# A 2x2 average pool: SP's load queue gets the first turn, and the last tile comes in two parts instead of three

## The chip, the cores and the metric

The kernel runs on one core of a Trainium2 chip. The metric is the device time of one execution in microseconds (us), lower is better. A kernel is executed several times. One of the executions is profiled, and its time is among those listed; the kernel before was profiled in an execution of its own (3104.99 us), which is in no list. The chips of the measurements differ and are told apart below as chips A to D (and the first measurement, whose chip is not named). The clock of the matrix engine, which is unused here, was granted at 1.0.

The engines are named as in the profile: DVE (VectorE) adds, ACT (ScalarE) scales and issues loads, POOL (GpSimd) issues stores, SP (SyncE) issues loads. Transfers run on 16 DMA engines, whoever issues them. A transfer waits in the queue of the engine that issued it; a *turn* is the time in which one DMA engine moves one piece (one packet) of one queue; and a transfer *lands* on a DMA engine when that engine reports its share as done.

## The reference, cut to what matters

```python
x: [32, 128, 256, 256] float32, kernel_size 2, stride 2
output[:, :, i, j] = mean over the 2x2 window of x          # [32, 128, 128, 128]
```

1073.7 MB are read and 268.4 MB written. There are three additions and one scaling per output.

## The kernel before

The input is 128 tiles of 32 "units" (a unit is two input rows per partition). A tile is loaded in two halves: SP loads its even partitions, ACT its odd ones, each 4 MB, one run of 65,536 bytes per partition. There are two tile buffers. DVE adds twice, ACT scales, and POOL stores two finished tiles at a time. Cuts are marked.

```python
    parts, a = [], 0
    while a < rest:                                  # rest is 32: the last tile
        b = rest if rest - a <= 8 else a + (rest - a) // 2
        parts.append((a, b, sem(f"part{len(parts)}")))   # 16, 8 and 8 units
        a = b

    def load(odd, k, b):
        (act if odd else sp).dma_start(out=ins[b][odd::2], in_=xp[b, odd][k]).then_inc(loaded[b], 16)
    ...
        for b in range(2):                           # SP
            load(0, 0, b)
        with sp.Fori(1, pairs) as k:
            for b in range(2):
                take(sp, free[b])
                load(0, k, b)
    ...
        for a, b, part in parts:                     # DVE, the last tile
            take(dve, part, 32)
            sums(it[:, a:b], dst[:, a:b])
    ...
        for b in range(2):                           # ACT
            load(1, 0, b)
        with act.Fori(0, (pairs - 1) // 2) as i:
            for c in range(2):
                for b in range(2):
                    next_load(b, load, 2 * i + (c + 1), b)
                    scale(both[c][:, b], scaled)
    ...
        for a, b, _ in parts:                        # ACT, the last tile
            take(act, summed)
            scale(dst[:, a:b], done)
            take(act, done)
            act.dma_start(out=block(...)[1], in_=dst[:, a:b]).then_inc(tail, 16)
```

Of the kernel before, what the change touches and what calls it, by code (L numbers as in the profile page):

```python
# [9 lines left out]
@with_exitstack  # L10
def kernel(
    ctx: ExitStack,
    tc: tile.TileContext,
    x: bass.AP,
    kernel_size: bass.AP,
    stride: bass.AP,
    out: bass.AP,
):
    nc = tc.nc
    P = nc.NUM_PARTITIONS  # L20

    n, c, h, w = x.shape
    k = int(kernel_size)
    s = int(stride)
    h_out = (h - k) // s + 1
    w_out = (w - k) // s + 1
    R = n * c * h_out
    units = R // P if R % P == 0 else 0


    if k == 2 and s == 2 and h % 2 == 0 and w == 256 and units >= 1024 and (units - 1) // 64 % 2 and (units - 1) // 32 % 2:
        _pool_2x2(ctx, tc, x, out, units)
    else:
        _generic_pool(ctx, tc, x, out, k, s, n, c, h, w, h_out, w_out)
# [5 lines left out]
def _pool_2x2(ctx, tc, x, out, units):  # L40
    nc = tc.nc
    P = nc.NUM_PARTITIONS
    f32 = mybir.dt.float32
    w = x.shape[3]
    w_out = w // 2
    sp, act, dve, pool = nc.sync, nc.scalar, nc.vector, nc.gpsimd

    xv = x.rearrange("n c (ho a) w -> (n c ho) (a w)", a=2)
    ov = out.rearrange("n c ho wo -> (n c ho) wo")









    in_pool = ctx.enter_context(tc.tile_pool(name="inp", bufs=2))
    out_pool = ctx.enter_context(tc.tile_pool(name="outp", bufs=2))  # L60
    ins = [in_pool.tile([P, TILE, 2 * w], f32, name="in_tile") for _ in range(2)]
    both = [out_pool.tile([P, 2, TILE, w_out], f32, name="res") for _ in range(2)]
    res = [both[t // 2][:, t % 2] for t in range(4)]

    def sem(name):
        return ctx.enter_context(nc.semaphore(name))

    loaded, free, stored, emptied = [
        [sem(f"{n}{b}") for b in range(2)] for n in ("loaded", "free", "stored", "emptied")
    ]  # L70
    halfway, summed, scaled, held, done, tail = [
        sem(n) for n in ("halfway", "summed", "scaled", "held", "done", "tail")
    ]



    def take(engine, sem, n=1):
        engine.wait_ge(sem, n)
        engine.sem_inc(sem, -n)  # L79

    def block(r0, g):
        rows = slice(r0, r0 + g * P)
        return xv[rows].rearrange("(p g) f -> p g f", p=P), ov[rows].rearrange("(p g) f -> p g f", p=P)

    pairs, rest = divmod(units - TILE - 1, 2 * TILE)
    whole, rest = 2 * pairs + 1, rest + 1
    assert pairs % 2 and pairs >= 5 and rest <= TILE
    last = 2 * pairs * TILE * P
    xp = xv[0:last].rearrange("(k o p t g) f -> t o k p g f", o=2, t=2, p=P // 2, g=TILE)
    op = ov[0:last].rearrange("(k o p g) f -> o k p (g f)", o=2, p=P // 2, g=2 * TILE)  # L90
    parts, a = [], 0
    while a < rest:
        b = rest if rest - a <= 8 else a + (rest - a) // 2
        parts.append((a, b, sem(f"part{len(parts)}")))
        a = b

    def load(odd, k, b):
        (act if odd else sp).dma_start(out=ins[b][odd::2], in_=xp[b, odd][k]).then_inc(loaded[b], 16)

    def load_block(odd, dst, r0, g, landed):  # L100
        (act if odd else sp).dma_start(out=dst[odd::2], in_=block(r0, g)[0][odd::2]).then_inc(landed, 16)

    def load_last(odd):
        for a, b, part in parts:
            load_block(odd, ins[whole % 2][:, a:b], (whole * TILE + a) * P, b - a, part)

    def sums(it, dst):
        dve.tensor_add(out=it[:, :, 0:w], in0=it[:, :, 0:w], in1=it[:, :, w:]).then_inc(halfway)  # L108
        take(dve, halfway)
        dve.tensor_add(out=dst, in0=it[:, :, 0:w:2], in1=it[:, :, 1:w:2]).then_inc(summed)  # L110

    def tile_sums(t):
        if t % 2 == 0:
            take(dve, emptied[t // 2 % 2])
        take(dve, loaded[t % 2], 32)
        sums(ins[t % 2], res[t % 4])

    def scale(dst, sem):
        act.mul(out=dst, in_=dst, mul=0.25).then_inc(sem)  # L119

    def next_load(b, *what):

        take(act, summed)
        act.sem_inc(free[b])
        what[0](1, *what[1:])



    def store_from(engine, k, c, landed):
        for o in range(2):  # L130
            src = both[c][o::2].rearrange("p t g f -> p (t g f)")
            engine.dma_start(out=op[o][k], in_=src).then_inc(landed, 16)  # L132

    def store(k, c):
        take(pool, scaled, 2)
        store_from(pool, k, c, stored[c])

    def emptied_by(c, landed):
        pool.wait_ge(stored[c], landed)
        pool.sem_inc(emptied[c])  # L140

    with tc.tile_critical():

        for b in range(2):
            load(0, 0, b)
        with sp.Fori(1, pairs) as k:
            for b in range(2):
                take(sp, free[b])
                load(0, k, b)
        take(sp, free[0])  # L150
        load_block(0, ins[0], last, TILE, loaded[0])
        take(sp, free[1])
        load_last(0)
        take(sp, held, 2)
        c = (pairs - 1) % 2
        store_from(sp, pairs - 1, c, tail)


        for b in range(2):
            dve.sem_inc(emptied[b])  # L160
        with dve.Fori(0, whole // 4):
            for t in range(4):
                tile_sums(t)
        for t in range(whole - whole % 4, whole):
            tile_sums(t)
        it = ins[whole % 2]
        dst = ins[(whole + 1) % 2].rearrange("p g (s f) -> p (g s) f", s=4)[:, 0:TILE]
        for a, b, part in parts:
            take(dve, part, 32)
            sums(it[:, a:b], dst[:, a:b])  # L170


        for b in range(2):
            load(1, 0, b)
        with act.Fori(0, (pairs - 1) // 2) as i:
# [4 lines that stand above are left out]
        c = (pairs - 1) % 2  # L180
        next_load(0, load_block, ins[0], last, TILE, loaded[0])
        scale(both[c][:, 0], held)
        next_load(1, load_last)
        scale(both[c][:, 1], held)
        take(act, summed)
        scale(res[(whole - 1) % 4], done)
        take(act, done)
        act.dma_start(out=block(last, TILE)[1], in_=res[(whole - 1) % 4]).then_inc(tail, 16)
        for a, b, _ in parts:
# [3 lines that stand above are left out]
            act.dma_start(out=block((whole * TILE + a) * P, b - a)[1], in_=dst[:, a:b]).then_inc(tail, 16)  # L193


        store(0, 0)
        with pool.Fori(0, (pairs - 3) // 2) as i:
            for c in (1, 0):
                store(2 * i + (2 - c), c)
                emptied_by(1 - c, 32 * i + 32)  # L200
        store(pairs - 2, 1)
        for c in range(2):
            emptied_by(c, 16 * (pairs - 1))
        pool.drain()


        take(sp, tail, 16 * (len(parts) + 3))
# [95 lines left out]
```

## Time and profile before

| | before |
|---|---|
| time, median of the first 3 executions | 3107.12 us (3106.73 to 3108.3) |
| profiled execution, its span | 3104.99 us, 3103.3 us |
| DVE, ACT, POOL busy | 54%, 16%, 2% |
| DMA | 90% or more in each of 40 slices, mean 433 GB/s |

The prediction below shows the lines for this, those of the timeline with start, duration, engine, line, operation, operands, idle time before it. The page's list of DMA queues names the queue, its packets, its megabytes, and its share of the 16 engines' time; q1 is SP's queue, q10 ACT's, and q0 the software queue of POOL:

```profile
q10 hardware_dynamic: 10976, 541.07, 40.3%
q1 hardware_dynamic: 10560, 541.07, 40.2%
q0 software_dynamic: 9920, 260.05, 19.4%
```

The shares add up to 99.9%: there is no room between the packets. And the timeline (start, duration, engine, line, operation, operands, idle time before it) shows when DVE can begin, which is when the first tile has landed:

```profile
23.56 8.69 DVE L108 TENSOR_TENSOR in_tile<-in_tile 128x8192 f32<-128x8192 f32 x1 [23.56 <-DVEq L79]
```

### The profile page before, as it was taken

The numbers are of one execution on the slowest core, as the hardware profiler recorded it, in microseconds if no ns is written. First come the engines' busy times: TensorE is split into PE (matmuls) and PEld (weight loads), VectorE is DVE, ScalarE is ACT, GpSimd is POOL, SyncE is SP. The second block draws the span as 40 slices with busy tenths as digits, with TensorE's granted clock in tenths as the row PEclk, the third lists the DMA queues.
The fourth block names the chain that finished last, engine by engine and source line by source line (L and its number), as shares of the span: only waits on it lengthen the run. The fifth ranks groups of instructions, "written<-read, shape, count | busy, mean of one in ns | idle before, by whom it ended". The sixth has DMA issues, their size and how long they took to land. (4 is left out here: it accounts for less than half of the span.)

```text
span 3103.3 us, 2911 instructions
## 1 busy us (share of the span) xinstructions
DVE 1679.3 (54%) x260; ACT 503.0 (16%) x161; POOL 67.2 (2%) x128
## 2 busy tenths in 40 slices
DVE  5555655556555565555655555555555555555555
ACT  1111112111121111211111111111111111111111
POOL 0000000000000000000000000000000000000000
DMA  9999999999999999999999999999999999999999
GB/s 419 427 438 433 439 426 439 435 430 433 438 427 438 438 426 433 435 439 429 439 427 439 433 439 426 439 431 434 433 439 426 439 437 428 432 433 440 431 439 393
DMA packets 31457, 1342.21 MB, mean 433 GB/s; under 512 B 6240, under 2 KB 6240, under 8 KB 6496
## 3 DMA queue, kind: packets, MB, share of 16 engines
q10 hardware_dynamic: 10976, 541.07, 40.3%
q1 hardware_dynamic: 10560, 541.07, 40.2%
q0 software_dynamic: 9920, 260.05, 19.4%
q14 instruction: 1, 0.01, 0.0%
HBM read 1073.74 MB, written 268.44 MB: 432 GB/s over the span
## 5 line engine op out<-in xcount | busy, mean ns | idle before, releaser
L108 DVE TENSOR_TENSOR in_tile<-in_tile 128x8192 f32<-128x8192 f32 (+1 forms) x130 | 1112.9, 8561 | 1393.3 <-DVEq L79 1393.3
L119 ACT ACTIVATE res<-res 128x4096 f32<-128x4096 f32 x127 | 459.2, 3616 | 1849.3 <-ACTq L79 1829.3
L110 DVE TENSOR_TENSOR res<-in_tile 128x4096 f32<-128x4096 f32 x127 | 562.0, 4425 | 18.6
L119 ACT ACT_TABLE_LOAD x31 | 39.8, 1283 | 733.2 <-ACTq L79 733.2
L132 POOL DMA_DIRECT2D out_dram<-res x124 | 67.0, 540 | 2942.3 <-POOLq L79 2939.5
L119 ACT ACTIVATE in_tile<-in_tile 128x1024 f32<-128x1024 f32 (+1 forms) x3 | 4.0, 1341 | 7.3 <-ACTq L79 7.3
L110 DVE TENSOR_TENSOR in_tile<-in_tile 128x1024 f32<-128x1024 f32 (+1 forms) x3 | 4.7, 1580 | 0.4
L284 POOL MEMSET const-float32-0.0<- 128x1 f32 x1 | 0.1, 93 | 0.4 <-issue 0.4
L284 POOL MEMSET const-bfloat16-1.0<- 128x1 bf16 x1 | 0.1, 95 | 0.0
L284 POOL MEMSET const-float32-1.0<- 128x1 f32 x1 | 0.1, 93 | 0.0
L284 POOL MEMSET const-uint8-127<- 128x1 uint8 x1 | 0.1, 93 | 0.0
## 6 DMA issues: line engine op xcount, KB each, us to landing
out_dram<-res POOLq DMA_DIRECT2D x124, 2048.0 KB, 42.0
out_dram<-res SPq DMA_DIRECT2D x2, 2048.0 KB, 32.4
in_tile<-in_x_dram ACTq DMA_DIRECT2D x1, 2048.0 KB, 16.9
in_tile<-in_x_dram SPq DMA_DIRECT2D x1, 2048.0 KB, 20.5
in_tile<-in_x_dram ACTq DMA_DIRECT2D x2, 1024.0 KB, 25.0
in_tile<-in_x_dram SPq DMA_DIRECT2D x2, 1024.0 KB, 25.1
out_dram<-res ACTq DMA_DIRECT2D x1, 2048.0 KB, 14.2
in_tile<-in_x_dram ACTq DMA_DIRECT2D x127, 30.9
```

The lines of the kernel that those rows point to most:

```text
L108: dve.tensor_add(out=it[:, :, 0:w], in0=it[:, :, 0:w], in1=it[:, :, w:]).then_inc(halfway)
L110: dve.tensor_add(out=dst, in0=it[:, :, 0:w:2], in1=it[:, :, 1:w:2]).then_inc(summed)
L119: act.mul(out=dst, in_=dst, mul=0.25).then_inc(sem)
L132: engine.dma_start(out=op[o][k], in_=src).then_inc(landed, 16)
L284: nc = _bacc.Bacc("TRN2", target_bir_lowering=False, num_devices=1)
```

## The change

The intent is that SP's queue gets the first turn on the DMA engines, and that the end has fewer, larger pieces.

```diff
-    halfway, summed, scaled, held, done, tail = [
+    halfway, summed, scaled, held, done, tail, first = [
 ...
-        b = rest if rest - a <= 8 else a + (rest - a) // 2
+        b = rest if rest - a <= 16 else a + (rest - a) // 2
 ...
         for b in range(2):
             load(0, 0, b)
+            if b == 0:
+                sp.sem_inc(first)
 ...
+        take(act, first)
         for b in range(2):
             load(1, 0, b)
```

More of the change, by code (lines that the diff above doesn't have):

```diff
@@ L70, in _pool_2x2 @@
     ]
-    halfway, summed, scaled, held, done, tail = [
-        sem(n) for n in ("halfway", "summed", "scaled", "held", "done", "tail")
+    halfway, summed, scaled, held, done, tail, first = [
+        sem(n) for n in ("halfway", "summed", "scaled", "held", "done", "tail", "first")
     ]
```

## The prediction

> **What bounds the kernel now.** I read the page first, for the engines and the DMA rows:
>
> ```profile
> DVE 1679.3 (54%) x260; ACT 503.0 (16%) x161; POOL 67.2 (2%) x128
> ...
> DMA  9999999999999999999999999999999999999999
> ...
> DMA packets 31457, 1342.21 MB, mean 433 GB/s; under 512 B 6240, under 2 KB 6240, under 8 KB 6496
> ```
>
> No compute engine is over 54% busy, and the 16 DMA engines are at 90% or more in all 40 slices. To see whether a little is still lost between the nines, I asked the view of windows for two stretches of 193.4 us, the loop's period of eight tiles. Its columns are the window, its length, the busy times of DVE, ACT and POOL, the clock, the DMA share, and GB/s:
>
> ```profile
> 500.00:693.40 193.40, 104.94 (x16) 31.49 (x10) 4.32 (x8) 1.00 1.00 434
> 1500.00:1693.40 193.40, 104.85 (x17) 31.50 (x10) 4.32 (x8) 1.00 1.00 434
> ```
>
> The share is 1.00 both times, at the same 434 GB/s. A load puts one piece of 65,536 bytes per partition row on an engine. 434 GB/s over 16 engines is 27.1 GB/s each, so a piece takes 65,536 / 27.1e9 = 2.42 us, which is also what nearly every such packet lasts in the trace. The whole job is 1342.2 MB / 16 / 65,536 = 1280 such turns per engine, and 1280 x 2.417 us = 3094 us. That leaves about 9 us of the 3103.3 us span for start and end, and only there can the change act.
>
> The start, in the timeline and the windows:
>
> ```profile
> 1.06 1.21 ACTq L98 DMA_DIRECT2D in_tile<-in_x_dram  x2
> 1.10 1.44 SPq L98 DMA_DIRECT2D in_tile<-in_x_dram  x2
> ```
>
> ```profile
> 0.00:2.40 2.40, 0.00 (x0) 0.00 (x0) 0.20 (x4) 1.00 0.00 0
> 2.40:5.40 3.00, 0.00 (x0) 0.00 (x0) 0.00 (x0) 1.00 1.00 350
> ```
>
> ACT issues 0.04 us ahead of SP. Nothing moves before 2.4 us, about 1.36 us after that issue. The next 3.0 us carry 350 GB/s x 3.0 us = 1.05 MB, exactly one piece per engine, and the packet records put all 16 pieces on ACT's queue; SP's first begin at 5.45 us. So ACT has the first turn by 0.04 us of issue, and SP's first piece waits a turn.
>
> The end, in the windows and the timeline:
>
> ```profile
> 3096.00:3098.00 2.00, 0.00 (x0) 0.00 (x0) 0.00 (x0) 1.00 0.99 408
> 3098.00:3100.00 2.00, 0.00 (x0) 0.00 (x0) 0.00 (x0) 1.00 0.09 37
> 3100.00:3102.00 2.00, 0.00 (x0) 0.00 (x0) 0.00 (x0) 1.00 0.05 20
> ```
>
> ```profile
> 3077.66 4.42 DVE L108 TENSOR_TENSOR in_tile<-in_tile 128x4096 f32<-128x4096 f32 x1
> ...
> 3082.22 2.29 DVE L110 TENSOR_TENSOR in_tile<-in_tile 128x2048 f32<-128x2048 f32 x1
> ...
> 3084.43 2.28 DVE L108 TENSOR_TENSOR in_tile<-in_tile 128x2048 f32<-128x2048 f32 x1
> 3084.64 1.91 ACT L119 ACTIVATE in_tile<-in_tile 128x2048 f32<-128x2048 f32 x1 [3.16 <-ACTq L79]
> ...
> 3090.44 1.23 DVE L110 TENSOR_TENSOR in_tile<-in_tile 128x1024 f32<-128x1024 f32 x1
> 3091.79 1.06 ACT L119 ACTIVATE in_tile<-in_tile 128x1024 f32<-128x1024 f32 x1 [2.52 <-ACTq L79]
> 3092.95 0.34 ACTq L193 DMA_DIRECT2D out_dram<-in_tile  x1
> ```
>
> Full rate holds until 3098 us; then about 3.5 us follow at 37 and 20 GB/s, the rate of one engine. The record of landings (one update per DMA and engine) says why: in each of the last loads and stores 15 engines land together and one lands 3.3 to 4.5 us after them. That one's lag grows slowly, from below 0.1 us over the next engine at 90 us to about 3 us at 2890 us. It is still at work on its backlog when the others are through, and its last packets follow one another without a hole until 3101.6 us; the last landing is at 3102.0 us and the span ends at 3103.3 us. **The end is therefore set by the backlog of one DMA engine**, not by the chain DVE, ACT, store, although the last store was issued 9.1 us before it landed. I therefore do not rely on the chain of waits: it sees only the last 1.1 us of ACT.
>
> **What the Trainium skill says.** The page "DMA: Bandwidth & Descriptors", section Specifications, gives a fabric ceiling of 435 GB/s; the trace runs at 434, so it agrees and nothing is left to gain in the middle. Its section "Queues, rings and completion order" says that each engine goes round robin over the queue rows that have work, at packet granularity; the trace agrees, with alternate pieces of ACT's and SP's queue, 2.42 us each. Its "Rules for kernel authors" says that spreading DMAs over issuing engines brings no bandwidth, since all run on the same 16 engines. That tells against any gain from who goes first. The page "VectorE: DVE Perf Modes" has fp32 tensor_tensor at one element per cycle of 0.96 GHz: 4096 elements are 4.27 us, the trace has 4.42, so I may scale by length.
>
> **The change, first part: SP first.** Added are an increment on SP after its first issue, and a wait with a decrement on ACT. From the two issues in a row (1.06 and 1.67 on ACT, 1.10 and 1.72 on SP), one issue takes SP about 0.6 us. SP then issues at 1.10, signals near 1.7, and ACT issues near 1.8 us, some 0.75 us later than now. With the same 1.36 us to the first byte, SP's first pieces begin at 2.46 us instead of 2.42: **+0.04 us** on the path. ACT's are ready at 1.8 + 1.4 = 3.2 us and have their turn only when SP's first piece is through, near 5.5 us, so 2.3 us of slack swallow the delay. ACT's second load, now issued near 2.4 us, is wanted after the whole first tile, near 22 us. Tile 0 needs both halves and both land about where they do now, with their order swapped. In the steady loop all engines stay at 1.00 and the order of turns moves no bytes: **0**.
>
> **Second part: two parts of 16 units instead of 16, 8 and 8.** Three things change. On DVE, the second and third parts now cost 4.42 + 2.29 in one go instead of 2 x (2.28 + 1.23), and one pair of gaps between instructions goes. The second part starts at 3084.43 as now (its data, the former second and third part, landed by 3082.6 on the slowest engine). Its second add then begins at 3084.43 + 4.42 + 0.14 = 3088.99 and ends at 3091.28 instead of 3090.44 + 1.23 = 3091.67: -0.39. On ACT the last scale takes 1.91 instead of 1.06, so the last issue goes from 3092.95 to 3091.28 + 0.12 + 1.91 + 0.10 = 3093.41: +0.46. And the last store is 1024 KB instead of 512 KB: 64 KB per engine, 2.4 us of data instead of 1.2. If the last store were exposed, this would be 0.46 + 1.2 = +1.7 us. It is not. Taking 1.5 us from issue to first packet, it is ready at 3094.9. The 15 engines are busy with earlier work, the 2048 KB and the first 1024 KB, until about 3096, and the late one until 3099.1. So it is hidden by 1 us on the many and by 4 us on the one that sets the end. The total bytes are the same. What remains is the packets' own cost: rows of 4 KB follow each other every 0.155 us, rows of 8 KB last 0.309, so 16 of the former (2.48) against 8 of the latter (2.46) save 0.02 us on the late engine, and a few semaphore packets of 0.01 us go: **about -0.05 us**.
>
> **Sum:** +0.04 - 0.05, hence zero: 3107.1 becomes 3107.1 us.
>
> **Rivals.** (a) *The last store comes onto the path* (+1.7 us, about 3108.8), if in unprofiled runs the engines empty earlier than in this trace. Against it: the share of 0.99 up to 3098. (b) *ACT's wait opens a hole at the start*: if the signal from SP took over 2.3 us longer than I think, each engine would idle after SP's first piece, were SP's second and third not already queued behind it. They are, so even this costs nothing in throughput, at most up to 2 us in the first tile's landing, which DVE's spare time absorbs. (c) *The late engine lags differently with swapped turns*: its lag is the one term of 3 us that I can't derive. Nothing in the profile ties it to the order of the queues, since it grows through stretches where the order never changes; but if it vanished, the time would be about 3103.5, and if it doubled, 3110.5. (d) *Fewer parts shorten a bound tail*: DVE ends 0.39 us sooner; this would count only if DVE set the end, and the 9.1 us to the last landing say it doesn't.
>
> **Range and chances.** The three timings of before span 1.6 us, and the profiled execution took 3105.0, 2.1 us below their median; that scatter is larger than every effect above. I keep the point at the median, 3107.0 us after rounding, and take 3104.8 to 3109.2 us for 8 in 10: the scatter, with rival (a) inside the upper half and part of (c) inside the lower. Two per cent is 62 us, twenty times any rival, so: faster 0.01, same 0.98, slower 0.01.
>
> **What would show it.** First packets on SP's queue near 2.45 us, ACT's issue near 1.8 us with its pieces from about 5.5 us: first part right. DMA share 1.00 and 434 GB/s in the loop's windows: no gain in the middle. A last issue near 3093.4 us, a last landing near 3102, and one engine alone at the end: second part hidden. Wrong I am if the windows of the last 15 us show a share clearly below 0.9 before the last store's data, if the lag of the one engine is gone or doubled, or if the last landing moves by over 2 us while the loop stays the same.

## The result, and the profile after

| | before | after |
|---|---|---|
| executions, us | 3107.12, 3106.73, 3108.30, 3104.84 | 3104.58 (profiled), 3101.72, 3101.53, 3101.85 |
| median, us | 3106.93 | 3101.78 |
| span of the profiled execution | 3103.3 | 3102.8 |

The ratio is 0.9986, with a 95% interval from 0.9969 to 1.0003. A ratio is the mean time of one kernel's runs over that of the other's of the same rounds, so it is not quite the ratio of the medians. Executions over 1.5% slower than the fastest of the same kernel are left out of the means. The median is 5.2 us lower, under the range that was predicted. The table already holds the puzzle: the profiled execution after is only 0.4 us faster than the profiled one before, and the executions that nobody watched are 3 us faster than that.

First the profile. The page after, for the engines and the DMA rows:

```profile
DVE 1679.2 (54%) x258; ACT 503.0 (16%) x160; POOL 67.5 (2%) x128
...
DMA  9999999999999999999999999999999999999999
...
DMA packets 31152, 1342.20 MB, mean 433 GB/s; under 512 B 6192, under 2 KB 6192, under 8 KB 6192
```

DVE has two instructions less, and the 256 packets of 4 KB from the two small stores are gone (under 8 KB was 6496). The windows in the loop (columns as in the prediction) are those of before:

```profile
500.00:693.40 193.40, 104.94 (x16) 31.50 (x10) 4.34 (x8) 1.00 1.00 434
1500.00:1693.40 193.40, 104.80 (x17) 31.50 (x10) 4.34 (x8) 1.00 1.00 434
```

The start, in the timeline:

```profile
1.10 38.95 SPq L98 DMA_DIRECT2D in_tile<-in_x_dram  x3
1.82 38.20 ACTq L98 DMA_DIRECT2D in_tile<-in_x_dram  x3
...
25.89 8.69 DVE L108 TENSOR_TENSOR in_tile<-in_tile 128x8192 f32<-128x8192 f32 x1 [25.89 <-DVEq L79]
```

ACT issues at 1.82 us, as worked out. But DVE begins 2.33 us later than before. The packet records say why: SP's first pieces start at 2.45 us, and ACT's at 7.82 us, not at 5.5. SP got two turns in a row, although ACT's load had been issued 3.6 us before the second of them began. In the long run it costs nothing: by the fourth tile the landings differ by 0.2 us from those before.

The end, in the timeline and then in the windows:

```profile
3084.18 4.42 DVE L108 TENSOR_TENSOR in_tile<-in_tile 128x4096 f32<-128x4096 f32 x1
...
3088.75 2.29 DVE L110 TENSOR_TENSOR in_tile<-in_tile 128x2048 f32<-128x2048 f32 x1
3091.17 1.91 ACT L119 ACTIVATE in_tile<-in_tile 128x2048 f32<-128x2048 f32 x1 [4.87 <-ACTq L79]
3093.18 0.34 ACTq L196 DMA_DIRECT2D out_dram<-in_tile  x1
```

```profile
3096.00:3098.00 2.00, 0.00 (x0) 0.00 (x0) 0.00 (x0) 1.00 0.95 401
3098.00:3100.00 2.00, 0.00 (x0) 0.00 (x0) 0.00 (x0) 1.00 0.10 41
3100.00:3102.00 2.00, 0.00 (x0) 0.00 (x0) 0.00 (x0) 1.00 0.03 12
```

The last issue is at 3093.18 us, and again 15 engines are through by about 3098.8 us and one works alone; its last landing is at 3101.64 us, against 3102.02 before. So the end of the profiled execution went as predicted. What must be explained is the other three.

**How the one engine falls behind.** In the profile before I looked at how long packets last. Nearly all last the same: 2.418 us for a piece of 64 KB of a load, 1.213 us for one of 32 KB of a store. After 100 us, 200 of these two kinds last 4 ns or more longer, and their excess adds up to 3.14 us (1.90 us in the store packets of POOL's queue, 0.15 us in SP's, 1.08 us in ACT's loads). That is close to the lag at the end, 3.3 us. After 1200 us there are 109 such packets, and all 109 start at least 0.2 us after the packet of their queue before them, as one in eight of all packets there does: the late engine's, and the first of the bunch in which the others start. So one engine loses some 16 ns at a time on average, some 200 times, and it does not catch up: the DMA share is 1.00 throughout the loop. After the change the same sum is 2.83 us, and the lag at the end 2.8 us.

**What time a run without the lag would take.** Before, the time minus the last landing is 3104.99 - 3102.02 = 2.97 us. The 15 engines' last landing is at 3098.69 us; with this as the end, the time would be 3101.66 us. After, it is 3098.84 + (3104.58 - 3101.64) = 3101.78 us. The three unwatched executions after are at 3101.53 to 3101.85 us. By their times they look like executions without the late engine. The experiments test which part of the change brings them, and whether this reading holds.

### The profile page after: what moved, and what is told of

Same layout as the page of the kernel before. It is cut to its first block, busy times and chain, and to the rows that moved or that the text cites. A ratio compares the mean times of both kernels' runs of the same rounds, so it can differ in the third digit from the quotient of the medians.

```text
span 3102.8 us, 2903 instructions
## 1 busy us (share of the span) xinstructions
DVE 1679.2 (54%) x258; ACT 503.0 (16%) x160; POOL 67.5 (2%) x128
## 5 line engine op out<-in xcount | busy, mean ns | idle before, releaser
L108 DVE TENSOR_TENSOR in_tile<-in_tile 128x8192 f32<-128x8192 f32 x129 | 1112.8, 8626 | 1393.0 <-DVEq L79 1393.0
```

The lines of the kernel that those rows point to most:

```text
L108: dve.tensor_add(out=it[:, :, 0:w], in0=it[:, :, 0:w], in1=it[:, :, w:]).then_inc(halfway)
```

## The experiments

The runs came in batches, four kernels in most; those of one batch shared their chip and the executions of the kernel before. The ratios of all of them, but those of the runs on half of the rows, lie between 0.9983 and 1.0005 with 1 inside every interval, since single executions of 3114 to 3135 us, which come with either start and still count, widen them. So I read the single executions; the profiled one is set apart in each list. Any chip's kernel before, in 55 executions, was at 3104.14 us at the least, with a median of 3104.99 us.

### Each part alone, the change again, and the noise (chip A)

e1, the first part alone:

```diff
 (the whole change, but)
-        b = rest if rest - a <= 16 else a + (rest - a) // 2
+        b = rest if rest - a <= 8 else a + (rest - a) // 2
```

> The first part alone: SP's first issue before ACT's, the last tile still in three parts. Theory A (chance: neither part acts, and the 5 us between the medians are scatter between executions and chips): ratio to the kernel before within 0.0005 of 1, that is within 1.5 us. Theory B (the order of the first turns changes how far the one late DMA engine falls behind): 3 to 5 us shorter than before, about 3102 us, like the whole change. Theory C (the two larger parts shorten the end): as before, within 1 us. In the profile the first pieces of ACT begin near 7.8 us under all three.

e2, the second part alone:

```diff
 (the kernel before, but)
-        b = rest if rest - a <= 8 else a + (rest - a) // 2
+        b = rest if rest - a <= 16 else a + (rest - a) // 2
```

> The second part alone: two parts of 16 units, ACT still first. Theory A: within 1.5 us of before. Theory B: within 1 us of before, about 3107 us if the kernel before is there again. Theory C: 3 to 5 us shorter, about 3102 us. In the profile the last issue should be near 3093.4 us and the late engine alone at the end under all three.

e3 is the change without an edit:

> The whole change once more, with more rounds, on the same chip as its two halves. Theory A: within 1.5 us of before. Theories B and C: 3 to 5 us shorter than before, as in the first measurement (3101.8 against 3106.9 us).

e4 is the kernel before with a comment:

```diff
-TILE = 32
+TILE = 32  # as before
```

> The kernel before with one comment added, so the same instructions: the noise of this comparison itself. All theories: ratio 1 within its interval. If it differs from before by over 1.5 us, differences of that size between kernels mean nothing here, which is Theory A's case; if it stays within 0.5 us, a difference of 3 us is real.

Measured:

```
                    profiled   unprofiled
e1 first part       3106.69    3102.58 3101.69 3105.53 3101.91
e2 two parts        3104.45    3105.08 3104.28 3104.62 3105.54
e3 the change       3108.58    3101.69 3101.84 3118.04 3125.87 3101.70
e4 before, comment  3105.77    3104.78 3177.44 (slow) 3104.84 3104.59 3104.29
before              10 executions, 3104.14 to 3106.78, and one of 3135.46
```

The second part alone does nothing: 3104.62 us in the median, against 3104.79 of before. With the first part, with or without the second, some executions fall to 3101.7 to 3101.9 us (five of nine unprofiled ones; I call this the low mode), and none of the others do. Theory C falls, and Theory A in its plain form too: the noise is large, but it has a floor, and the first part lowers the floor by 2.5 us. Theory B names the right part; its mechanism is not shown by this.

### The mirror, a longer delay, and half of the work (chip B)

All the kernels of this batch end in three parts, like the kernel before. m1, ACT first and SP waiting:

```diff
+        take(sp, first)
         for b in range(2):
             load(0, 0, b)
 ...
         for b in range(2):
             load(1, 0, b)
+            if b == 0:
+                act.sem_inc(first)
```

> The mirror: SP waits until ACT has issued its first load; three parts at the end. In the four runs so far the unprofiled times of the two kernels with SP first lie at 3101.5 to 3102.6 us in seven of eight undisturbed cases, those with ACT first at 3104.1 to 3106.8. Theory S (it matters that the two first issues do not meet, whichever goes first): here also 3101.5 to 3102.6. Theory P (it matters that SP's queue and not ACT's has the first turns): 3104.1 or more, as before.

m2 is e1, the first part alone, but SP signals after its second load instead of its first, so that ACT waits longer:

```diff
-            if b == 0:
+            if b == 1:
                 sp.sem_inc(first)
```

> ACT waits until SP has issued both of its first loads, near 2.4 us, so its first piece comes a turn or more later still. Theories S and P: 3101.5 to 3102.6 us, as with SP first. Theory N (what helps is that the first tile lands one turn later, a shift of the compute against the transfers): the time changes again, by a turn of 2.4 us or part of it, in either direction.

The half runs (wrong results, half of the output stays unwritten), of the kernel before and of e1:

```diff
-        _pool_2x2(ctx, tc, x, out, units)
+        _pool_2x2(ctx, tc, x, out, units // 2)
```

> The kernel before on half of the rows (wrong result on purpose, half of the output stays unwritten), so 32 loop periods of 48.34 us fewer, 1546.9 us. To be read against its counterpart with SP first. Theory F (with ACT first one turn of 2.4 to 2.7 us is lost once, at the start or the end): 3104.4 - 1546.9 = 1557.5 us, 2.7 us over the counterpart. Theory D (one engine loses a little in every period): 1556.2 us, 1.3 us over the counterpart.

> SP first, three parts at the end, on half of the rows (wrong result on purpose). Both theories: 3101.7 - 1546.9 = 1554.8 us. The difference to the counterpart with ACT first tells: 2.7 us for a turn lost once (F), 1.3 us for a drift over the run (D).

Measured:

```
                      profiled   unprofiled
m1 ACT first          3104.15    3104.57 3104.85 3104.74 3105.97
m2 SP both first      3104.82    3104.00 3107.43 3107.14 3104.66
half, ACT first       1556.81    1556.87 1556.51 1556.48 1556.47
half, SP first        1556.45    1556.48 1558.04 1556.55 1556.37
before                9 executions, 3104.38 to 3107.42
```

No execution reaches the low mode, neither in the mirror nor with SP issuing both loads. That speaks against Theory S, and against SP's first turn as such (P) too. The two halves agree within 0.1 us, which fits neither F (2.7 us apart) nor D (1.3 us). This batch was inconclusive: the change itself was not in it, so it could not tell a start that doesn't help from a chip on which no start helps. The start of e1 was in it only on half of the rows.

### Stores without the software queue (chip C)

More than half of the late engine's excess lies in packets of POOL's queue. So in hw_act and hw_sp SP and ACT issue the loop's stores themselves, half each (hw_sp has the start of e1; both end in three parts):

```diff
 (SP, at the end of each pair of tiles; ACT alike with the odd half, after its two scales)
+                take(sp, ready)
+                half_store(sp, 0, 2 * i + c, c)
 (POOL)
-                store(2 * i + (2 - c), c)
```

> The whole change once more, on whatever chip this batch gets. So far: 3101.5 to 3101.9 us in its undisturbed unprofiled executions on the first chip and on the next, before at 3104.1 to 3108.3 there. On the third chip only relatives were run (SP issuing both loads first: 3104.0 to 3107.4, no gain). Theory K (the gain of 2.7 us belongs to this exact start): 3101.5 to 3101.9 here again, before 3104 or more. Theory X (it belongs to the chip): no difference to before within 1 us.

> The first part alone once more, three parts at the end. It should go as the whole change does on the same chip under both theories (K: 3101.5 to 3102.6 us; X: as before), since the parts at the end have shown no effect; a difference of over 1 us between the two would speak against that.

> ACT first as before, but in the loop the stores are issued by SP and ACT, a half each, behind their loads; GpSimd issues none. If the one late engine is late because of the stores' software queue (Theory Q), the late engine's lag of about 3 us at the end should go, and the time should be 3101.7 us or a little less, whatever the start. If the lag has another cause, it stays in the trace, and the time is at 3104 or more.

> The same stores with SP first. Theory Q: as its counterpart with ACT first within 0.5 us, about 3101.7. If the start acts by itself, also without a software queue (Theory K in its strict form): 2 to 3 us less than the counterpart.

e5 is the whole change and e6 the first part alone, both again without an edit. Measured:

```
                             profiled   unprofiled
e5 the change                3104.52    3101.70 3113.73 3106.52 3101.34 3101.51
e6 first part                3107.49    3104.74 3105.41 3104.47 3101.70
hw_act stores by SP, ACT     3106.90    3107.33 3106.85 3106.47 3106.47
hw_sp  the same, SP first    3106.36    3107.27 3106.71 3106.54 3107.08
before                       11 executions, 3104.39 to 3107.42
```

The low mode is there on this chip: three executions of e5 and one of e6. Theory X, in the form that only one chip has it, falls. The expectation of e6, that the first part alone should go as the whole change does, was not met: the unprofiled medians are 3104.61 and 3101.70 us, apart by more than the 1 us that I had named as speaking against it. On the two chips where both ran, the low mode came in 6 of 10 unprofiled executions of the whole change and in 3 of 8 of the first part alone. That is too few to say whether the second part makes it more frequent, and it is not excluded. The stores by SP and ACT made it worse by 2 us, with no mode at all, so what Theory Q expected, 3101.7 us without a lag, did not come: the end of hw_act's profile, in its windows, has more engines late, not fewer.

```profile
3098.00:3100.00 2.00, 0.00 (x0) 0.00 (x0) 0.00 (x0) 1.00 0.99 412
3100.00:3102.00 2.00, 0.00 (x0) 0.00 (x0) 0.00 (x0) 1.00 0.53 219
3102.00:3104.00 2.00, 0.00 (x0) 0.00 (x0) 0.00 (x0) 1.00 0.12 49
```

Here 219 GB/s still flow between 3100 and 3102 us, where the kernel before has 20. By the packet records all 16 engines still move data at 3100 us, six at 3101 to 3102 us and two at 3103 us; in the kernel before one is left from 3098.5 us on. So this edit brings a cost of its own on all engines. It shows that engines are late without the software queue too; it does not show what the one late engine would do if only that queue were gone. The expectation for a start that acts by itself, 2 to 3 us between the two, isn't met either: their medians are 0.1 us apart.

### The change, the mirror and the longer delay on one chip (chip D)

f1 is the change, f2 is m1, f3 is m2, f4 is the half run with SP first, without a new edit. Note that f2 and f3 end in three parts and f1 in two, so f3 differs from f1 in two things.

> The whole change, on the same chip as its two relatives below. If the mode belongs to the start: at least two of the unprofiled executions at 3101.3 to 3101.9 us, as on three chips so far. If the third chip was simply one without the mode and this is such a chip: all at 3104 or more.

> The mirror, ACT first and SP waiting. If who goes first matters: 3104 us or more in all executions while the change shows 3101.3 to 3101.9. If only a clean separation of the two first issues matters: the low mode here too, where the change has it.

> SP issues both of its loads first. If SP's first turn is what matters: the low mode, as the change. If it takes the exact timing of ACT's first load 0.7 us after SP's: 3104 us or more, as on the other chip.

> SP first on half of the rows (wrong on purpose). If the mode is a gain at the start or the end, executions at 1554.6 us (3101.5 - 1546.9) appear where the change shows its mode. If it is a lag that builds up late in the run and is then avoided or not: 1556.4 to 1556.6 us as before, since half of the run doesn't get that far.

Measured:

```
                      profiled   unprofiled
f1 the change         3107.58    3125.51 3101.48 3101.72 3101.86 3101.73
f2 ACT first          3104.51    3104.61 3104.58 3105.66 3104.78
f3 SP both first      3104.66    3108.68 3105.89 3105.92 3104.85
f4 half, SP first     1556.69    1554.78 1554.82 1556.51 1554.85
before                11 executions, 3104.19 to 3108.44
```

Now the three starts stand side by side. On this chip the low mode comes with the start of the change, and with neither relative in four unprofiled executions each. The fairer partner for f3, the first part alone, is not in this batch; with the same three parts it is f4, half of the run, that shows the low mode here, in three of four (and g2 below in three of four more). What tells f3 from the change at the start is a small thing, seen in the timelines (f3's first, then the mirror's):

```profile
1.10 1.20 SPq L98 DMA_DIRECT2D in_tile<-in_x_dram  x2
2.46 1.20 ACTq L98 DMA_DIRECT2D in_tile<-in_x_dram  x2
```

```profile
1.06 1.20 ACTq L98 DMA_DIRECT2D in_tile<-in_x_dram  x2
1.79 1.52 SPq L98 DMA_DIRECT2D in_tile<-in_x_dram  x2
```

In f3 ACT issues at 2.46 us instead of 1.82. Its first pieces start at 7.93 us, against 7.88 in f1, since SP has two turns first in both, and the first tile lands near 25.7 us in both. The mirror has the same spacing as the change with the queues swapped. In the undisturbed profiles the loop doesn't differ in anything that I could find, beyond how soon the late engine falls behind.

f1's profile is a warning of its own. Its end, in the windows:

```profile
3096.00:3098.00 2.00, 0.00 (x0) 0.11 (x1) 0.00 (x0) 1.00 0.56 233
3098.00:3100.00 2.00, 0.00 (x0) 0.00 (x0) 0.00 (x0) 1.00 0.81 332
3100.00:3102.00 2.00, 0.00 (x0) 0.00 (x0) 0.00 (x0) 1.00 0.12 49
3102.00:3104.00 2.00, 0.00 (x0) 0.00 (x0) 0.00 (x0) 1.00 0.10 41
```

The share drops to 0.56 before the last data: the last store was issued at 3096.21 us, 3 us later than in the first profile of the change, so most engines ran dry before it came, which is rival (a) of the prediction. Two engines then work on for over 3 us: 49 GB/s is nearly twice the 27 of one engine, and they land last at 3103.38 and 3104.64 us. This execution took 3107.58 us, 6 us more than its unprofiled neighbours of the low mode. All six profiled executions with the change's start took 3104.52 to 3108.58 us. A profile of the low mode was never caught. Four of these six (e1, e3, e6, f1) are disturbed: their longer packets, counted as above, add up to 11 to 31 us, most of it after 2300 us, against 2.5 to 7.5 us in the whole-run profiles of the other starts that keep POOL's stores. So only two profiles, the first one and e5, show the change's start undisturbed, and both have one late engine.

### The two halves on one chip (chip D again)

> ACT first on half of the rows (wrong on purpose), beside its counterpart. If the low mode belongs to the start: 1556.4 us or more in every execution, as before. If it belongs to the chip: 1554.8 here too, wherever the counterpart has it.

> SP first on half of the rows (wrong on purpose). If the low mode belongs to the start and comes and goes by execution: some at 1554.8 us, as on the last chip. If none again, as on the chip before that, the chip decides whether this start helps.

```
                      profiled   unprofiled
g1 half, ACT first    1556.50    1557.43 1556.19 1556.57 1556.43
g2 half, SP first     1556.44    1556.86 1554.92 1554.82 1554.72
before                6 executions, 3104.20 to 3106.70, and three of 3115.95 to 3131.15
```

On one chip, half of the run with SP first has the low mode and with ACT first it has not. So the mode is not the chip's alone. But on chip B the same half run never showed it in four unprofiled executions, which suggests that the start alone doesn't bring it either.

The size of the gain tells its kind. The low mode is at 1554.82 us in half of the run (median of six) and at 3101.70 us in the whole one (median of 16). The difference is 1546.9 us. A loop period is 48.337 us by the landings of the stores on the 15 engines in the profile before (2803.54 us over 58 periods), and 32 of them are 1546.8 us. So in the low mode the second half of the run takes, within 0.1 us, what its packets take on an engine that isn't late. With ACT first the difference is 3104.99 - 1556.49 = 1548.5 us, 1.7 us more than its packets, and the late engine in the profile before fell 1.4 us further behind over that half (from 1.73 us at 1540 us to 3.15 at 3014). And the gap between the modes in half of the run, 1.7 us, is what the profile of half_act shows as its late engine's lag: the last landing is at 1553.84 us, the last of the others at 1552.16 us. A turn lost once at the start or the end (Theory F) would have made both gaps equal.

## Why the prediction was right or wrong

**What bounds the kernel: right.** The share stays 1.00 at 434 GB/s in the loop, and the end is set by the backlog of one DMA engine. The low mode at 3101.7 us fits the time that the other 15 engines would set.

**First part, the start: partly wrong.** SP's first piece at 2.45 us and ACT's issue at 1.82 us came as worked out. That ACT's pieces would follow near 5.5 us did not: they came at 7.8 us, since SP had two turns. The tile therefore landed 2.3 us later, not at about the same time. Rival (b) had said that even such a delay would cost nothing, and it did cost nothing.

**Second part: right.** The last issue was expected at 3093.41 us and was at 3093.18, and the last landing stayed near 3102. The part alone (e2) moved the median by 0.2 us. One product is rounded wrongly: 8 rows of 0.309 us are 2.47 us, so the rows save 0.01 us and not 0.02. And rival (a), the last store coming onto the path, did happen in one profiled execution, f1's.

**The step that failed is the sum for the first part,** "In the steady loop all engines stay at 1.00 and the order of turns moves no bytes: 0". It is true of the bytes and of the first profile, and wrong for most of the unprofiled executions, which are 3.3 us shorter. What it leaves out, as far as the sizes tell, is the term that sets the end: the lag of the late engine. I had named it as rival (c), given it 3 us, and dismissed it because "Nothing in the profile ties it to the order of the queues". Across all chips, 16 of 26 unprofiled executions with the change's start are below 3102 us, and not one of 72 unprofiled executions with ACT first (17 of e2, e4, m1 and f2, one of which is slow, and 55 of before) is below 3104.1. The profile could not have shown it, because no profiled execution fell into that mode.

**The base was off, too.** I took 3107.1 us, the median of three executions. Over 55 executions the median is 3104.99 us. So of the 5.2 us between the first medians, some 2 us are the scatter of before, and 3.3 us (3104.99 to 3101.70) the mode. The same error made my figure for a vanished lag, 3103.5, too high: it should have been the profiled time less its lag, 3104.99 - 3.3 = 3101.7 us, which could be had from the profile before.

**What is shown and what stays open.** Shown: the low mode comes with the first part, and never in 72 executions with ACT first, the mirror among them; the second part alone brings nothing; the gain is larger in the whole run than in half of it; engines are late without the software queue of the stores, too. Likely, on few executions: that a longer delay loses the mode (0 of 8 unprofiled executions of m2 and f3, against 3 of 8 of the first part alone on other chips, and 6 of 8 of its half run on chip D). Argued from sizes that agree within 0.3 us, but not seen: that the low mode is an execution in which no engine drifts behind. Open: whether the second part makes the mode more frequent, why ACT's first load 0.7 us behind SP's brings the low mode in some executions while 1.4 us (f3) did not, what the single longer packets wait for, and why chip B showed no low mode in the half run. I have no theory for these that a run supports.

## What to carry to other kernels

When every DMA engine is busy from start to end, look at which engine lands last, not only at the mean share: the last landing of the 15 others gave here, within 0.3 us, the time of the best executions. Compare the time of the profiled execution with those of the unprofiled ones before explaining a few microseconds from a profile, and take the scatter of a kernel from many executions before predicting against it. An effect near 0.1% needs the single executions side by side; here means and intervals saw nothing of a mode that the sorted list shows at once.

## What the Trainium skill lacked or had wrong

- "DMA: Bandwidth & Descriptors", section "Queues, rings and completion order", says an engine alternates between the rows that have work. The trace agrees in the loop, but at the start SP's queue had two turns in a row (from 2.45 and from 5.40 us) although ACT's load had been issued 3.6 us before the second. That would fit a choice of the next turn that is made about a turn ahead, which no run here tests; the page doesn't say when the choice is made.
- The same page, section "Specifications", gives about 0.6 us to the first byte for loads issued by SP or ACT. Here the first packet started 1.36 us after the start of the issue (1.06 to 2.42 us) and 0.79 us after its end, since the issue itself took 0.57 us. The page doesn't say from which of the two it counts.
- The same page, section "Latency and other measured facts", has it that two of the engines are usually slower, and offers as a best guess contention from the descriptors of the software queue. Here one engine is late, by 3.1 us in 200 packets that are 16 ns too long on average, 1.90 us of it in the packets of that queue. With the loop's stores off that queue, more engines were late and the time rose to 3106.4 to 3107.3 us, which neither confirms nor excludes the guess for the one engine. The traces don't tell which engine it is.
- No page says that such a lag has two modes that depend on the start (3101.7 against 3104.1 us or more), nor that a profiled execution may never show the better one (0 of 6, against 16 of 26 unprofiled).
